# Attention: exponentials times values as one plain float32 matmul in place of three on split parts

## The chip, the cores and the metric

The kernel runs on one core of one Trainium2 chip. The metric is the device time of one execution in microseconds (us), lower is better. A core has TensorE (PE in the profile, with its weight loads as PEld), VectorE (DVE), ScalarE (ACT), GpSimd (POOL) and SyncE (SP), which here issues the DMAs. Each engine works through its own instructions in order; semaphores join them.

## The reference

A trunk of two layers on 512 latent and 256 context tokens of 1024 channels. In each layer one input projection feeds three mixers (a delta rule called RWKV-7, multi-head latent attention, an mLSTM); their outputs go through one output projection, then a SwiGLU network. All of it is float32. What the change touches is the softmax attention of 8 heads, with 96 channels for keys and queries and 64 for values:

```python
def attend(q, keys, vals):
    s = jnp.einsum('bhqd,bhkd->bhqk', q, keys).astype(jnp.float32) * (MLA_QK ** -0.5)
    p = jax.nn.softmax(s, axis=-1)
    return jnp.einsum('bhqk,bhkd->bhqd', p.astype(vals.dtype), vals)
...
    keys = jnp.concatenate([kl, kc], axis=2)
    vals = jnp.concatenate([vl, vc], axis=2)
    out = lax.map(lambda q_blk: attend(q_blk, keys, vals), qb)
...
    if ctx_out:
        oc = attend(qc, kc, vc)
```

Latent queries see all 768 keys, context queries the 256 context keys. Layer 1 has no context output.

## The kernel before

Most large matmuls are done on split operands: a float32 number is held as a high and a low part of type float32r, 12 significant bits each, and a product is three matmuls: high by high, high by low, low by high (the helper mm3, and the loop in gemm at line 263). The projections, the feed-forward network and both matmuls of attention work so. The delta rule and the mLSTM use plain float32 matmuls.

Within a layer come, in this order: the first norm, the input projection with the delta rule, the mLSTM with the attention's up-projections beside it (mla_up), the attention (mla_attend), the output projection (add, on pages of y), the second norm and the feed-forward network.

In mla_up keys and queries are made by token, normalised, rotated, transposed and sent to DRAM by head. At its end the values are made: for each of 6 tiles of 128 tokens the up-projection's PSUM tile (up) is copied by ScalarE to a high part (line 974) and subtracted by VectorE to a low part (line 975). A head has 96 columns of a value tile, 64 of values and 32 of ones (zeros in the low parts), so that the sum of a query's weights comes out of the same matmul.

In mla_attend a head's keys and queries are loaded and split (load, tiles k; lines 996 to 1000), one head ahead. The maximum of each query's scores is taken first (maxima): a matmul on the high parts alone into tile mx (line 1014), a reduction by VectorE into mr (line 1016), a transpose by matmul into pt (line 1020), and a copy by ScalarE into row 96 of the queries (line 1021), so that the scores come out with the maximum subtracted. Then attend goes over the key tiles, 6 for latent queries (512 columns) and 2 for context queries (256 columns, layer 0 alone): three matmuls for the scores (tile st, lines 1034 to 1036, two PSUM buffers), the exponential on ScalarE (line 1038, tile pe), the exponential's split (lines 1040 and 1041), and three matmuls into po (lines 1043 to 1045), which gathers a head's output over its key tiles. In even tiles VectorE copies and subtracts; in odd tiles ScalarE copies and GpSimd subtracts (the patterns in SPLIT). At the end of a range the sums go through a transpose, a reciprocal and a broadcast transpose (lines 1050 to 1058), and VectorE multiplies the outputs (line 1061, tile y).

The maxima of the next head are woven in between the key tiles, two steps for each (the generator ahead), and one step of the delta rule's output (rwkv_post, tiles yt, ph, pst; lines 751 to 782) follows each head but the last. Within these dependencies the order on each engine is made by the framework, which schedules the whole program on a simulated time line before it is built; an edit in one place can so move instructions in others. Layer 0 has 8 x (6 wide + 2 narrow) tiles of exponentials, layer 1 has 8 x 6 wide ones, 112 in all.

Of the kernel before, what the change touches and what calls it, by code (L numbers as in the profile page):

```python
# [24 lines left out]
SPLIT = ('va', 'vg')  # L25
QN = 2
EB = 3
# [18 lines left out]
PARTS = (8, 7, 7)     # hidden tiles taken at a time  # L46
# [6 lines left out]
# tiles of the input projection: 0-1 r, 2-3 k, 4-5 v, 6 wd, 7 ad, 8 gd | 9-12 cq, 13-14 ckv,  # L53
# 15 rotary key and gates | 16 q, 17 k, 18-19 v, 20-21 o
N_IN = 22

# columns of the per-channel parameters
# [9 lines left out]
# the modulation's tiles: on TensorE (layer 0), on VectorE  # L67
MOD_PE = [m for k in range(5) for m in (k, KD + k)]
MOD_DVE = [(0, m) for m in range(48) if m not in MOD_PE] + [(1, m) for m in range(48)]
FIRST = (0, 1, 2, 5, 3, 6, 4, 7)      # the order of the first norm's pages  # L70


def constants():
# [6 lines left out]
    # decay products of the delta rule: rows are key tokens s, columns (P | R) query tokens t  # L80
# [11 lines left out]
    # the upper right quarters of the diagonal blocks of 32 and 64  # L92
    lev = [(s // l == t // l) & (s % l < l // 2) & (t % l >= l // 2) for l in (32, 64)]
    c["c_lev"] = np.tile(np.stack(lev, 1), (2, 1, 1)).astype(f)
    # partition 32 g + 4 q + b holds column block b of row block 2 (g % 2) + i: masks of the diagonal ones
# [16 lines left out]
def pack(inp):  # L112
# [4 lines left out]
    def cm(w, width=P):  # L117
        """[..., K, M] -> [..., M / width, 128, K / 128, width]"""
        *b, K, M = w.shape
        w = w.reshape(*b, K // P, P, M // width, width)  # L120
        n = len(b)
        return np.ascontiguousarray(w.transpose(*range(n), n + 2, n + 1, n, n + 3))

    def km(w):
        """[..., K, M] -> [..., 128, K / 128, M]"""
# [16 lines left out]
    # the delta rule's output channels go (head parity, head pair, channel)  # L142
# [35 lines left out]
def trunk(ctx, tc, I, out, dbg=None):  # L178
# [35 lines left out]
    def rsqrt(dst, src, w, tag):  # L214
        """dst = src ** -0.5 for [128, w] float32 tiles: a step of third order, then one of Newton's"""
# [5 lines left out]
        ve.scalar_tensor_tensor(dst, t, 5.0, dst, ALU.add, ALU.mult)       # 8 / 3 of the root  # L221
# [4 lines left out]
    def split(hi, lo, src, en=ve):  # L226
        """src = hi + lo, both in 12 significant bits"""
# [3 lines left out]
    def weight(src, k, m, en=ve):  # L231
        """[128, k, m] weights from DRAM, as their two parts"""
# [7 lines left out]
    def pages(n, order=None):  # L240
        """n pages of 768 tokens, each in two parts"""
# [3 lines left out]
    def mm3(o, a, b, start, stop):  # L245
        """o += a^T b for split operands"""
# [4 lines left out]
    KORD = (0, 1, 6, 7, 2, 3, 4, 5)     # attention comes last  # L251
# [4 lines left out]
    def gemm(pool, parts, act, ranges, order=None):  # L256
        """W^T act by ranges of tokens: (psum, first, last); parts: [(hi, lo, first k)], act[k] = (hi, lo)"""
# [9 lines left out]
    def gemm_both(pools, ws, act, order):  # L267
        """two output tiles' W^T act over all tokens, page by page of act: their [(psum, first, last)]"""
# [17 lines left out]
    def mod_pe(k, wk, bufs, pool):  # L286
        """layer 0's shift and scale of page k on TensorE"""
# [16 lines left out]
    def silu_rows(wk, pm):  # L304
        """silu(c), silu(c_ctx) on all partitions"""
# [10 lines left out]
    def mod_dve(l, m, cb, t, wk, bufs):  # L316
        """a layer's projection m of c on VectorE"""
# [7 lines left out]
    def gain(l, which, a=0, b=KD):  # L325
        """g * (1 + scale) of one of a layer's two norms, pages a to b"""
# [5 lines left out]
    def norm_stat(acc, X, k, a, b, tmp, en):  # L332
        """acc += the squares of X's page k"""
# [7 lines left out]
    def norm_scale(acc, rng, pm, tag="ss", bufs=1):  # L341
        """1 / rms of ranges of tokens, on all partitions: [(psum, first, last)], and the last operation"""
# [18 lines left out]
    def norm_page(l, which, X, h, bc, k, a, b, tmp):  # L361
        """the modulated norm of X's page k, tokens a to b, into the split page of h"""
# [15 lines left out]
    def pads(z):  # L378
        """the zeros around the latent (1-512) and the context tokens (514-769)"""
# [3 lines left out]
    def shift(t, z, u, c, n):  # L383
        """t += c * (left neighbour + right neighbour)"""
# [12 lines left out]
    def joint(a0, a1):  # L397
        """the like views a0 and a1 of one tile as one view, [partitions, 2, ...]"""
# [3 lines left out]
    def rwkv_in(l, ctx_out, h, rp, rq, tp, pm, pc, early, each):  # L402
        """the projection's tiles for the delta rule, shifted; unit keys, values by token, bonus"""
# [437 lines left out]
    def mla_up(l, ctx_out, lat, wk, vp, pm, krt, post, marks):  # L841
# [123 lines left out]
        for vs, x in ((his, 1.0), (los, 0.0)):  # L965
            for v in vs:
                gp.memset(v[:, :, :, 64:96].bitcast(F32), x)
# [584 lines left out]
```

## Time and profile before

| | |
|---|---|
| median of 3 runs | 2311.01 us (2308.34 to 2317.83) |
| the profiled execution: span from first to last instruction | 2302.2 us |
| busy in it: TensorE, VectorE, ScalarE, GpSimd | 2157.2, 1474.2, 876.9, 381.9 us |
| as shares of the span | 94%, 64%, 38%, 17% |
| mean granted TensorE clock over the span | 0.956 |

The page gives the span of the profiled execution and no time of its own around it; the median of the runs is 8.8 us above the span, the lowest run 6.1 us. A granted clock of 1.0 is 2.4 GHz and 0.5 is 1.2 GHz, the two levels of TensorE's clock; values between are means over a stretch. A matmul's duration in the trace reaches over the start of the next, so a matmul's price is read from one start to the next, not from its duration. A plain float32 matmul of the program shows as two records, each with its weight load.

### The profile page before, as it was taken

The page shows a single profiled execution, that of the slowest core. Times are in us where ns is not written, and L with a number is a line of the kernel's source. Part 1 is how long each engine was busy: PE and PEld are TensorE (multiplying, and loading weights), DVE is VectorE, ACT ScalarE, POOL GpSimd, SP SyncE. Part 2 cuts the span into 40 slices and gives each one's busy share as a digit, 9 for nine tenths or more (in the row PEclk, how much of TensorE's full clock was granted, in tenths as well). Part 3 has the DMA queues.
Part 4 walks back from the last instruction along what each step waited for, and adds up shares of the span by engine and source line. Part 5 has one row for each costly group of instructions (what it writes and reads, how often), then busy time and mean ns, then how long its engine had stood idle before and what let it go on. Part 6 is the DMA issues. An engine that isn't in the chain of part 4 may idle for free.

```text
span 2302.2 us, 36903 instructions
## 1 busy us (share of the span) xinstructions
PE 2157.2 (94%) x14716; PEld 1804.8 (78%) x14716; DVE 1474.2 (64%) x2830; ACT 876.9 (38%) x1583; POOL 381.9 (17%) x544
## 2 busy tenths in 40 slices
PE   6999997987989999999999989999797998999999
PEld 3788886775778888888888878887685677888887
DVE  6687777986767766545444455788798855433333
ACT  4433333654653522122122254434474554222221
POOL 1022332333431100000000111123143421000000
PEclk9999997896899999999999999999797998999999
DMA  7341112231006244333432311211231122333333
GB/s 287 94 141 61 61 41 88 59 103 38 27 11 211 75 136 135 123 118 123 144 127 68 114 60 57 79 52 43 84 106 51 35 64 91 93 97 96 96 97 101
DMA packets 87355, 212.02 MB, mean 92 GB/s; under 512 B 10248, under 2 KB 33680, under 8 KB 86544
## 3 DMA queue, kind: packets, MB, share of 16 engines
q1 hardware_dynamic: 87184, 209.67, 28.6%
q8 instruction: 115, 1.88, 0.3%
q14 instruction: 56, 0.46, 0.1%
HBM read 187.62 MB, written 22.02 MB: 91 GB/s over the span
## 4 chain that ended last, share of the span: by engine, by line
PE 79%; DVE 13%; ACT 3%; DMA 3%; issue 2%; POOL 1%; SPq 0%; DVEq 0%; ACTq 0%; POOLq 0%
PE gm L263 57%; PE psm L586 2%; PE inv L661 2%; PE st L1034 1%; DVE cT L321 1%; DVE mr L1016 1%; PE st L1035 1%; PE mx L1014 1%; DVE wl L229 1%; PE st L1036 1%; PE psm L515 1%; PE po L1045 1%; PE pB L701 1%; DMA wd<-in_mod_d 1%; PE psm L574 1%
## 5 line engine op out<-in xcount | busy, mean ns | idle before, releaser
L263 PE MATMUL gm<-hpage,wh 128*128 128x512 f32 (+1 forms) x3744 | 994.6, 353 | 15.4 <-ACT hpage L228 10.6
L263 PEld LDWEIGHTS gm<-hpage,wh 128*128 128x128 f32 x3744 | 660.1, 190 | 118.2 <-ACT hpage L228 13.0
L263 PE MATMUL gm<-hpage,wl 128*128 128x512 f32 (+1 forms) x1872 | 654.2, 352 | 1.2 <-DVE wl L229 0.9
L228 ACT ACTIVATE wh<-wr 128x1024 fp32r<-128x1024 f32 (+2 forms) x214 | 221.6, 1036 | 556.2 <-PE gm L263 457.7
L263 PEld LDWEIGHTS gm<-hpage,wl 128*128 128x128 f32 x1872 | 355.4, 190 | 49.6 <-DVE wl L229 2.2
L229 DVE TENSOR_TENSOR wl<-wr,wh 128x1024 fp32r<-128x1024 f32 (+2 forms) x214 | 257.7, 1204 | 180.8 <-ACT wh L228 178.8
L263 PE MATMUL gm<-hid,wh 128*128 128x512 f32 (+1 forms) x1056 | 282.6, 356 | 0.0
L263 PEld LDWEIGHTS gm<-hid,wh 128*128 128x128 f32 x1056 | 185.5, 188 | 32.3
L263 PE MATMUL gm<-hid,wl 128*128 128x512 f32 (+1 forms) x528 | 187.4, 356 | 0.0
L1344 DVE SCALAR_TENSOR_TENSOR X<-gm,mod,X 128x512 f32<-128x512 f32 (+1 forms) x100 | 64.2, 643 | 192.0 <-PE gm L263 187.3
L321 DVE CUSTOM_DVE_ANT_0 cT<-wd,cB,mod_b 128x1024 f32<-128x1024 f32 x140 | 177.1, 1294 | 0.4
L1514 DVE SCALAR_TENSOR_TENSOR ft<-ft,gm 128x512 f32<-128x512 f32 x66 | 39.5, 598 | 153.2 <-PE gm L263 153.1
L339 POOL TENSOR_TENSOR acc<-acc,sq 128x512 f32<-128x512 f32 (+1 forms) x15 | 22.6, 1517 | 563.0 <-ACT sq L338 563.0
L263 PEld LDWEIGHTS gm<-hid,wl 128*128 128x128 f32 x528 | 99.0, 188 | 16.1
L1041 POOL TENSOR_TENSOR pe<-pe,pe 128x512 fp32r<-128x512 f32 (+1 forms) x56 | 71.1, 1270 | 135.4 <-ACT pe L1071 107.0
L228 ACT ACTIVATE hid<-ft 128x512 fp32r<-128x512 f32 x66 | 36.2, 549 | 130.5 <-DVE ft L1514 130.5
L1038 ACT ACTIVATE pe<-st 128x512 f32<-128x512 f32 (+1 forms) x112 | 62.8, 563 | 60.8 <-PE st L1036 52.5
L1016 DVE TENSOR_REDUCE mr<-mx 128x1 fp32r<-128x768 f32 (+1 forms) x80 | 67.6, 845 | 20.4 <-PE mx L1014 19.9
L1512 ACT ACTIVATE ft<-gm 128x512 f32<-128x512 f32 x66 | 33.9, 514 | 89.9 <-PE gm L263 89.9
L1014 PE MATMUL mx<-k,k 96*128 96x256 f32 (+1 forms) x144 | 48.6, 414 | 16.5 <-DVE mr L1016 15.4
L586 PE MATMUL psm<-pr,kb 64*128 64x128 f32 (+1 forms) x384 | 55.7, 300 | 1.6 <-POOL pr L556 1.0
L229 POOL TENSOR_TENSOR hpage<-hu,hpage 128x256 fp32r<-128x256 f32 (+1 forms) x32 | 31.9, 1000 | 149.5 <-ACT hpage L228 148.8
(438 smaller groups left out, 3472.0 us busy)
## 6 DMA issues: line engine op xcount, KB each, us to landing
wr<-in_ffn_in SPq DMA_DIRECT2D x88, 512.0 KB, 3.5
wd<-in_mod_d SPq DMA_DIRECT2D x86, 512.0 KB, 4.1
wr<-in_w_in SPq DMA_DIRECT2D x44, 512.0 KB, 3.6
wr<-in_ffn_out SPq DMA_DIRECT2D x34, 448.0 KB, 3.4
wr<-in_w_out SPq DMA_DIRECT2D x20, 512.0 KB, 3.6
wr<-in_ffn_out SPq DMA_DIRECT2D x16, 512.0 KB, 3.6
zs<-ze SPq DMA_DIRECT2D x26, 256.0 KB, 2.0
X<-in_xT SPq DMA_DIRECT2D x16, 384.0 KB, 6.1
```

What stands on the lines that cost most here:

```text
L228: ac.activation(hi, src, AF.Copy)
L229: return en.tensor_tensor(lo, src, hi.bitcast(F32), ALU.subtract)
L263: pe.matmul(ps, x[:, j], act[k][y][:, a:b], start=(i == 0 and n == 0), stop=(i == len(kl) - 1 and n == 2))
L321: ve.tensor_tensor_reduce(out=t[:, s], in0=w, in1=cb[:, s], scale=1.0, scalar=modb[:, l, m:m + 1], op0=ALU.mult, op1=ALU.add, accum_out=mo ...
L586: pe.matmul(pa[j][:, p, c], flat(kb[hr, d, p, c]), flat(pr[hr, d, p, c, 0:nq]), start=True, stop=True)
L661: i = pe.matmul(v8(o)[hr, q], a[hr, d, p, c], b[hr, d, p, c], start=True, stop=True)
L1014: pe.matmul(ps[:, a - k0:b - k0], qh[0:96, n * P:(n + 1) * P], kh[0:96, a:b], start=True, stop=True)
L1016: ve.tensor_reduce(mr[:, n - q0:n - q0 + 1], ps[:, :T - k0], AX.X, ALU.max)
L1038: ac.activation(e, ps, AF.Exp, scale=QK_SCALE)
L1041: engine(1)(el, e, eh.bitcast(F32), ALU.subtract)
L1344: return ve.scalar_tensor_tensor(X[:, m, a:b], ps, mods[l][:, 24 * which + 16 + m, s:s + 1], X[:, m, a:b], ALU.mult, ALU.add)
L1514: ve.scalar_tensor_tensor(t2, t2, 0.5, pup, ALU.mult, ALU.mult)
```

## The change

The split of the exponentials and of the values goes. The values are one float32 tile (three pages of the pool hpage in place of five and one of the pool vl, which goes too), with ones beside each head's 64 columns. A key tile's exponentials go straight into one float32 matmul with them. The exponentials' tile pe has six buffers in place of three, since the two parts beside it are gone. Comments are gone as well; line numbers move by a few. The core of the diff:

```diff
-SPLIT = ('va', 'vg')
 QN = 2
-EB = 3
+EB = 6
...
-        his = [hp.tile([P, 2, 8, 96], F32R, name="hpage") for _ in range(3)]
-        los = [vp.tile([P, 2, 8, 96], F32R, name="vlow")] + [hp.tile([P, 2, 8, 96], F32R, name="hpage") for _ in range(2)]
-        for vs, x in ((his, 1.0), (los, 0.0)):
-            for v in vs:
-                gp.memset(v[:, :, :, 64:96].bitcast(F32), x)
-        V = [(his[n // 2][:, n % 2], los[n // 2][:, n % 2]) for n in range(NT)]
+        vs = [hp.tile([P, 2, 8, 96], F32, name="hpage") for _ in range(3)]
+        for v in vs:
+            gp.memset(v[:, :, :, 64:96], 1.0)
+        V = [vs[n // 2][:, n % 2] for n in range(NT)]
         wt = up_weight("ukv", 2, 512, 1024)
         for n in range(NT):
             ps = up(ckv, wt, n, 512)
-            hi, lo = (v[:, :, 0:64] for v in V[n])
-            src, r = ps.rearrange("p (h b) -> p h b", h=8), rkv[:, n:n + 1]
-            ac.activation(hi, src, AF.Copy, scale=r)
-            ve.scalar_tensor_tensor(lo, src, r, hi.bitcast(F32), ALU.mult, ALU.subtract)
+            ac.activation(V[n][:, :, 0:64], ps.rearrange("p (h b) -> p h b", h=8), AF.Copy, scale=rkv[:, n:n + 1])
...
                 e = wk2.tile([P, 512], F32, name="pe", bufs=EB)[:, :w]
                 ac.activation(e, ps, AF.Exp, scale=QK_SCALE)
-                eh, el = (wk2.tile([P, 512], F32R, name=f"pe{i}", bufs=EB)[:, :w] for i in range(2))
-                engine(0)(eh, e)
-                engine(1)(el, e, eh.bitcast(F32), ALU.subtract)
-                vh, vl = (v.rearrange("p h c -> p (h c)")[:, v0:v0 + P] for v in V[kt])
-                pe.matmul(po[:, :w], vh, eh, start=(kt == kts[0]), stop=False)
-                pe.matmul(po[:, :w], vl, eh, start=False, stop=False)
-                pe.matmul(po[:, :w], vh, el, start=False, stop=(kt == kts[-1]))
+                v = V[kt].rearrange("p h c -> p (h c)")[:, v0:v0 + P]
+                pe.matmul(po[:, :w], v, e, start=(kt == kts[0]), stop=(kt == kts[-1]))
                 yield
...
-        vp = rstack.enter_context(pool(f"vl{l}", 1, "right"))
```

What the schedule makes of it is seen best at the seam between two heads of layer 0 on TensorE. Before (in this order pt<-c_id,yt, pt<-c_id,ph and pt<-wa,g are a step of the delta rule's output, mx a maximum's matmul, pt<-idr,mr its transposes, pt<-one,row the transposes of the sums, st scores, po products):

```order
L1014 MATMUL mx<-k_6699,k_6706 128x512
L1014 MATMUL mx<-k_6699,k_6706 128x256
L772 MATMUL pt<-c_id,yt 128x128
L773 MATMUL pt<-c_id,ph 128x128
L774 MATMUL pt<-wa,g_6059 128x128
L772 MATMUL pt<-c_id,yt 128x128
L773 MATMUL pt<-c_id,ph 128x128
L774 MATMUL pt<-wa,g_6059 128x128
L1045 MATMUL po<-pe_6817,hpage 128x512
L1014 MATMUL mx<-k_6699,k_6706 128x256
L1020 MATMUL pt<-idr,mr 128x128 x6
L1053 MATMUL pt<-one_79,row 128x1 x4
```

The changed kernel at the like seam of layer 0 on TensorE (its line 1008 is 1014 above, 1014 is 1020, 1034 the product, 1042 is 1053):

```order
L771 MATMUL pt<-c_id,yt 128x128
L772 MATMUL pt<-c_id,ph 128x128
L773 MATMUL pt<-wa,g_5996 128x128
L771 MATMUL pt<-c_id,yt 128x128
L772 MATMUL pt<-c_id,ph 128x128
L773 MATMUL pt<-wa,g_5996 128x128
L1034 MATMUL po<-pe,hpage 128x512 x2
L1008 MATMUL mx<-k_6641,k_6648 128x512
L1008 MATMUL mx<-k_6641,k_6648 128x256
L1014 MATMUL pt<-idr,mr 128x128 x6
L1008 MATMUL mx<-k_6641,k_6648 128x256
L1042 MATMUL pt<-one_79,row 128x1 x4
```

A pair of matmuls for a maximum has moved from ahead of the delta rule's step to right ahead of the six transposes, which take its result, and two whole products stand between that step and the maximum where one third of a product stood.

## Rows read from the trace of the kernel before

**Rows 1.** The page's 2nd part: granted clock, tenths, 40 slices of 57.6 us

```profile
PEclk9999997896899999999999999999797998999999
```

**Rows 2.** Stretches: length, busy us (instructions) by engine, granted clock, DMA share, GB/s

```profile
490.00:513.00 23.00, 19.27 (x101) 16.27 (x99) 22.17 (x73) 12.31 (x22) 8.77 (x14) 0.93 0.23 70
533.00:690.00 157.00, 140.29 (x647) 111.29 (x647) 115.56 (x198) 91.36 (x175) 60.90 (x51) 0.86 0.07 20
1750.00:1875.00 125.00, 108.12 (x469) 81.95 (x468) 99.12 (x146) 74.55 (x130) 54.59 (x42) 0.89 0.15 45
1812.00:1875.00 63.00, 55.27 (x276) 42.46 (x275) 50.79 (x72) 42.04 (x74) 27.40 (x22) 1.00 0.16 50
```

**Rows 3.** TensorE in order of time, layer 0: start, length in us

```profile
542.46 0.40 PE L1045 MATMUL po<-pe,hpage 128*128 128x512 f32 x1
542.69 0.39 PE L1043 MATMUL po<-pe,hpage 128*128 128x512 f32 x1
```

**Rows 4.** TensorE's waits, 533 to 690 us: total us, times, longest

```profile
PE po L1045 <- DVE pe L1041: 4.5, 4, 1.6
PE pt L1020 <- DVE ph L781: 2.8, 4, 0.8
PE mx L1014 <- DVE mr L1016: 2.8, 3, 1.8
PE pt L1020 <- DVE mr L1016: 2.1, 3, 1.3
```

**Rows 5.** The same view, 1750 to 1875 us

```profile
PE mx L1014 <- DVE mr L1016: 5.1, 5, 2.2
PE pt L1020 <- DVE mr L1016: 2.8, 1, 2.8
PE po L1045 <- DVE pe L1041: 2.5, 2, 1.8
```

**Rows 6.** VectorE's groups, 533 to 690 us: busy us, mean ns, idle before

```profile
L1016 DVE TENSOR_REDUCE mr<-mx 128x1 fp32r<-128x768 f32 x28 | 26.7, 952 | 5.0 <-PE mx L1014 4.7
L1041 DVE TENSOR_TENSOR pe<-pe,pe 128x512 fp32r<-128x512 f32 x24 | 17.3, 722 | 1.0
L1040 DVE CAST pe<-pe 128x512 fp32r<-128x512 f32 x24 | 16.4, 681 | 12.0 <-ACT pe L1038 10.4 <-PE po L1044 1.5
L1041 DVE TENSOR_TENSOR pe<-pe,pe 128x256 fp32r<-128x256 f32 x8 | 8.9, 1111 | 0.2
```

**Rows 7.** The same view, 1750 to 1875 us

```profile
L1041 DVE TENSOR_TENSOR pe<-pe,pe 128x512 fp32r<-128x512 f32 x24 | 23.2, 966 | 1.0
L1040 DVE CAST pe<-pe 128x512 fp32r<-128x512 f32 x24 | 13.4, 559 | 10.2 <-ACT pe L1038 10.0
```

**Rows 8.** In order of time, layer 0: one stall; in brackets idle before

```profile
651.11 2.08 DVE L1041 TENSOR_TENSOR pe<-pe,pe 128x256 fp32r<-128x256 f32 x1
...
653.25 0.39 PE L1045 MATMUL po<-pe,hpage 128*128 128x256 f32 x1 [1.57 <-DVE pe L1041]
```

**Rows 9.** Stretches as in rows 2: a start, and after that stall

```profile
533.00:541.00 8.00, 7.55 (x20) 6.09 (x20) 3.19 (x6) 3.08 (x6) 1.28 (x1) 0.50 0.00 0
655.00:657.00 2.00, 2.00 (x7) 1.62 (x6) 1.97 (x4) 0.60 (x1) 0.91 (x1) 0.50 0.00 0
```

**Rows 10.** Line 1043: durations ns min/median/max, first and last start, forms

```profile
L1043 PE MATMUL po<-pe,hpage x112: 279/396/629, 537.9 to 1871.0; 128*128 128x512 f32 x96, 128*128 128x256 f32 x16
```

**Rows 11.** TensorE in order of time, layer 1: the mLSTM's plain float32 scores

```profile
1679.00 1.02 PE L1270 MATMUL pss<-ze,hpage 128*128 128x512 f32 x2
1679.85 0.60 PE L1307 MATMUL pbc<-mva,kd 128*128 128x260 f32 x2
```

**Rows 12.** Line 975, the values' low parts, as in rows 10

```profile
L975 DVE SCALAR_TENSOR_TENSOR hpage<-up,rkvn,hpage x8: 740/744/751, 504.9 to 1734.0; 128x512 fp32r<-128x512 f32 x8
```

**Rows 13.** VectorE in order of time, layer 1: ends of two heads

```profile
1812.44 0.67 DVE L1061 TENSOR_TENSOR y<-y,pt 64x512 f32<-64x512 f32 x1
...
1875.11 0.69 DVE L1061 TENSOR_TENSOR y<-y,pt 64x512 f32<-64x512 f32 x1 [0.81 <-PE pt L1058]
```

More of the change, by code (lines that the diff above doesn't have):

```diff
@@ L839, in latent, with mla_up @@
         return parts, rs
-    def mla_up(l, ctx_out, lat, wk, vp, pm, krt, post, marks):
+    def mla_up(l, ctx_out, lat, wk, pm, krt, post, marks):
         steps = iter(POST)
@@ L1061, in attend @@
             done.append((i, ve.tensor_tensor(yo, yo, bc[hr, :w], ALU.mult)))
-        used = {}
-        def engine(use):
-            i = used[use] = used.get(use, -1) + 1
-            en = SPLIT[use][i % len(SPLIT[use])]
-            if use:
-                return {"v": ve, "g": gp}[en].tensor_tensor
-            return {"a": lambda o, x: ac.activation(o, x, AF.Copy), "v": ve.tensor_copy, "g": gp.tensor_copy}[en]
         ranges = ((0, 4, 0), (4, 6, 512))[:2 if ctx_out else 1]
@@ L1441, in trunk @@
             post = rwkv_post(l, ctx_out, data, y, wp2, psum)
-            V = mla_up(l, ctx_out, lat, wk, vp, pm, krt, post, marks)
+            V = mla_up(l, ctx_out, lat, wk, pm, krt, post, marks)
         lstack.close()
```

## The prediction, made before the changed kernel ran

> **What bounds the kernel now.** Read the page first, then the stages that the change touches. On the page the granted clock is full in most slices of 57.6 us; it dips in the seventh to eleventh (345 to 633 us) and again in the thirty-first (1727 to 1784 us), which are around the two attentions [rows 1]. The exponentials-times-values products are all in line 1043 and the two lines after it, so two stretches matter, 533 to 690 us (layer 0) and 1750 to 1875 us (layer 1) [rows 2]. Their mean granted clock is 0.86 and 0.89, and VectorE is busy 115.6 of 157 us and 99.1 of 125 us. TensorE is called busy 140.3 and 108.1 us, but that counts overlapping durations and half-clock work, so it does not say how much it needs.
>
> What it needs comes from start times. At the full granted clock, 2.4 GHz, a 512-column matmul on float32r parts starts 0.23 us after the one before it [rows 3]. A layer 0 head has 36 of them in scores and products (two lots of 6 tiles by 3), 12 with 256 columns, and maxima, transposes and the delta rule's steps beside them. By 0.23 us and its half for 256 columns, the 112 tiles' scores and products need 96 x 6 x 0.23 + 16 x 6 x 0.12 = 144 us, of the 282 us of the two stretches. The rest is the other matmuls, half-clock time and waits. The waits of TensorE show which: the third product waits for the VectorE subtraction of line 1041, the maxima and their transposes (lines 1014, 1020) wait for VectorE's reduction, and the transposes of line 1020 wait for a delta-rule step in tile ph [rows 4, 5]. VectorE works in order, so much of the wait for a reduction is a wait for what was queued ahead of it, and the split of the exponentials is a large part of that queue [rows 6, 7]. One stall shows the whole mechanism: a 256-column subtraction takes 2.08 us from 651.11, the product behind it starts at 653.25 after 1.57 us of idle, and two microseconds later the granted clock is 0.50 [rows 8, 9].
>
> **The change part by part.** The sum is made against the profiled execution, whose span is 2302.2 us. The median of the runs shown, 2311.0 us, lies 8.8 us above that span; I take this difference as unchanged and add the sum to the median. A measurement of this kernel tells 0.5% (11.6 us) from no change.
>
> *The product.* Each of 112 tiles (96 with 512 columns, 16 with 256) [rows 10] loses three float32r matmuls and gains one plain float32 matmul. The mLSTM scores of line 1270 are a plain float32 matmul of the same 128 x 128 by 128 x 512 shape: one is two records in the trace, and what follows starts 0.85 us after the first [rows 11]. So 0.85 against 3 x 0.23 = 0.69: +0.16 us per wide tile. 96 x 0.16 = 15.4, and 16 x 0.08 = 1.3 for the narrow ones, scaled by columns (an estimate): **+16.7 us** at full clock. At half clock everything doubles; at today's mean clocks about a quarter of the time is at half clock (1 - 0.86 = 0.14, half rate, so 28%), which makes it 21; I take 19 because I expect less half-clock time. The Trainium skill, FP8 and Floating Point Precision, section TensorE Precision Notes, says that true float32 takes four passes through the array, against one for the truncated form. By that rule a tile would cost 4 x 0.23 = 0.92, the price would be about 24 us at full clock in place of 16.7, and the sum below would end 7 us higher, near 2305; the same shape was timed in this run [rows 11], so the sum goes by that.
>
> *The exponentials' split.* ScalarE or VectorE no longer copies the exponentials to float32r, VectorE or GpSimd no longer subtracts. VectorE sheds 17.3 + 16.4 + 8.9 us in the first stretch and 23.2 + 13.4 in the second [rows 6, 7], 79 us together. None of it is a saving by itself: only what TensorE waited for is. Directly waited for: 4.5 us (four times) in layer 0 and 2.5 us in layer 1 [rows 4, 5]. These waits cannot happen any more: **-7**.
>
> *The queue on VectorE.* Waits for the reduction (tile mr): 2.8 + 2.1 us in layer 0, 5.1 + 2.8 in layer 1 [rows 4, 5], 12.8 in all. VectorE loses over a third of its work there, but the reduction's own 0.95 us [rows 6] stays between a maximum and its transpose. Bounds: 0 and 12.8; I take 60%: **-8**.
>
> *A wait that is added.* The order of TensorE at the head's seam, quoted ahead, now has a maximum right in front of the six transposes that need its reduction; two whole products stand ahead of that maximum and cover the wait for ph (2.8 us, four times, [rows 4]). In its place comes a reduction of 0.95 us, four times: 3.8 - 2.8 = **+1**. Behind it wait the next scores, which need row 96 of the queries from those transposes.
>
> *The clock.* Time lost at half clock: (1 - 0.86) x 157 = 22 and (1 - 0.89) x 125 = 13.8 us, 36 at most. Idle time is in that, and so is the low clock with which each attention starts (0.50 from 533 to 541 us, before any product is late [rows 9]); by an estimate, 4 us for each start and 6 for idle time, about 22 is left. A split stall brings a low stretch on [rows 8, 9]; others follow waits for the reduction. Bounds: 0 and 22; I take 60%, as for the queue that causes them: **-13.5**.
>
> *The values' split.* Twelve VectorE instructions of 0.74 us, eight of them in the row and four more on tile vlow [rows 12], 8.9 us, leave the stretch before attention, where VectorE was busy 22.2 of 23 us in layer 0 [rows 2]. Some of them lie beside TensorE's up-projections, so bounds 0 and 8.9; half: **-4.5**. Memsets of the low parts, two fewer pages and one fewer pool cost or give nothing: no wait on a page of the values is in any row that I read. Twice the buffers for the exponentials (3 to 6) give nothing either: with two PSUM tiles for the scores, ScalarE can't run further ahead.
>
> *Elsewhere* the order changes only by neighbours; the output projection after attention in layer 0 starts when attention ends, so what is won passes through.
>
> Sum: 19 - 7 - 8 + 1 - 13.5 - 4.5 = **-13 us**; 2311 - 13 = **2298**.
>
> **The rivals.** *No change* (0.33). The direct waits and the values' split give 7 + 4.5 us, the price is 19 + 1, and the reduction's wait and the low clock stay because their cause is the chain maximum, reduction, transpose, row of the queries, which the change doesn't touch: +8.5, 2319.5. Or half of the two 60% terms comes: -2, 2309. For it: the reduction's waits are the longest ones left in layer 1. Against it: VectorE's queue is where they are made.
>
> *Slower* (0.15). TensorE is already what bounds, and each head pays its 6 x 0.16 = 1 us. The place is the second half of layer 1's attention: from 1812.4 to 1875.1 five heads end [rows 13], 12.5 us each at a granted clock of 1.00 [rows 2], where scores, products and maxima alone take 36 x 0.23 + 4 x 0.35 = 9.7 (a maximum is one matmul of 512 columns and one of 256). There the change costs about 5 us and has 3 to give back. If the first halves go the same way, 21 is paid at today's clock, the direct waits turn into waits for the reduction at the seams (+4 more), and only the values' 4.5 comes back: +20.5, 2331. It decides when the queue and the clock together return 8.5 us: there the change breaks even, and each us less is a us slower.
>
> *Much faster* (0.12 of the 0.52 below). All the waits go and the clock stays full: 16.7 - 7 - 12.8 - 22 - 8.9 = -34, 2277; the low clock at each start may shorten as well, by up to the 4 us each, so down to about 2268. Against it: the reduction's 0.95 us stays, and at the seam the order now puts it between two neighbours on TensorE.
>
> **How the numbers follow.** My forecast with the much faster case has 0.52, no change 0.33, slower 0.15; the forecast is over the 0.5% by little, which is why no change has a third. The range, 2268 to 2320, runs from the much faster end to the upper end of no change, leaving out most of the slower case and a little of the faster.
>
> **What would show it.** Right: line 1034 of the changed kernel has 224 records with starts 0.43 us apart; the granted clock of the two attention stretches rises over 0.92; layer 0's attention is shorter by 8 to 12 us and layer 1's first three heads by most of the rest, while the last five get no shorter; no TensorE wait names a subtraction of exponentials. Wrong: the clock stays at 0.86 and 0.89 with waits for the reduction as long as before (then no change), or the product's starts lie 0.46 us apart or more, or the last five heads of layer 1 grow by more than 1 us each (then slower).

## The result, and the profile after

The changed kernel takes 2280.8 us (median of 4 runs, 2277.9 to 2283.6) beside 2309.7 us of the kernel before (4 runs, 2303.9 to 2317.8). The ratio is 0.9868, 95% interval 0.9847 to 0.9890: 1.3% faster, 29 us, where 13 were forecast. The profiled execution of the changed kernel is its slowest of the four and that of before was its fastest, so the two spans, 2302.2 and 2281.8 us, lie only 20.4 us apart. The 8.8 us between span and median before, which the prediction took as fixed, are mostly this: that run took 2303.9 us, 1.7 above its span.

The page of the changed kernel, its granted clock and two groups (line 1010 is the reduction, 1016 before; 1034 the product):

```profile
PEclk9999997897999999999999989999697998999999
...
L1010 DVE TENSOR_REDUCE mr<-mx 128x1 fp32r<-128x768 f32 (+1 forms) x80 | 67.9, 848 | 83.8 <-PE mx L1008 83.6
L1034 PE MATMUL po<-pe,hpage 128*128 128x512 f32 (+1 forms) x224 | 112.2, 590 | 0.5 <-ACT pe L1032 0.4
```

The reduction's group before:

```profile
L1016 DVE TENSOR_REDUCE mr<-mx 128x1 fp32r<-128x768 f32 (+1 forms) x80 | 67.6, 845 | 20.4 <-PE mx L1014 19.9
```

There are 224 records for 112 products, and next to nothing is waited for in front of them. VectorE now sits idle for 83.6 us until a maximum comes from TensorE, where it was 19.9. The two attentions of the changed kernel, from the first scores to the first matmul of the output projection, columns as in [rows 2]:

```profile
533.86:673.20 139.34, 131.27 (x595) 91.50 (x596) 68.99 (x137) 76.00 (x148) 25.04 (x19) 0.97 0.08 22
1738.44:1855.36 116.92, 110.49 (x424) 70.90 (x425) 58.44 (x100) 60.69 (x106) 22.34 (x18) 0.93 0.16 48
```

The same two stretches of the kernel before, by the same marks:

```profile
533.45:693.21 159.76, 142.83 (x659) 113.06 (x660) 116.14 (x201) 93.72 (x180) 60.90 (x51) 0.86 0.07 19
1749.24:1874.76 125.52, 108.64 (x471) 82.19 (x469) 99.49 (x147) 74.55 (x130) 54.59 (x42) 0.89 0.15 45
```

Layer 0's attention is 20.4 us shorter and layer 1's 8.6, 29.0 together, as much as the medians lie apart; from one profile of each kernel, that it fits so closely is luck. VectorE's work in them falls from 215.6 to 127.4 us, and the granted clock goes from 0.86 and 0.89 to 0.97 and 0.93. Between the two attentions the changed kernel took 1065.2 us and the kernel before 1056.0; in the profiles of the twelve kernels below that stretch takes 1058.6 to 1076.1, so those 9 us are what hides a part of the gain in the two spans. But for the values' split of layer 1 the engines do the same work there; the granted clock is 0.98 before and 0.96 in the changed kernel, and why it differs is not shown.

TensorE's waits in the two attentions of the changed kernel (533 to 673, 1738 to 1855 us; total us, times, longest), beside [rows 4, 5]:

```profile
PE pt L1014 <- DVE mr L1010: 3.4, 6, 0.9
PE st L1028 <- ACT k L1015: 1.9, 3, 0.8
PE mx L1008 <- DVE mr L1010: 1.1, 2, 0.9
...
PE st L1028 <- ACT k L1015: 2.3, 6, 0.9
PE pt L1042 <- ACT row L1039: 1.8, 6, 0.7
PE pt L1014 <- DVE mr L1010: 0.9, 2, 0.5
PE mx L1008 <- DVE mr L1010: 0.6, 1, 0.6
```

The first three lines are layer 0's, the others layer 1's. The waits for the reduction were 12.8 us and are 6.0, or 5.1 without 0.9 that lies ahead of the first scores, and none is longer than one reduction; those of the transposes for the delta rule's step, and those for a subtraction of exponentials, are gone. The price of the product is near the forecast's 0.85 us. In order of time on TensorE, two products a key tile apart, at full clock:

```profile
541.71 1.02 PE L1034 MATMUL po<-pe,hpage 128*128 128x512 f32 x2
...
543.27 1.02 PE L1034 MATMUL po<-pe,hpage 128*128 128x512 f32 x2
```

They start 1.56 us apart; with three scores at 0.23 us, 0.69 in all, 0.87 is left for a product. VectorE in layer 1, ends of two heads, beside [rows 13]:

```profile
1790.38 0.67 DVE L1050 TENSOR_TENSOR y<-y,pt 64x512 f32<-64x512 f32 x1
...
1854.70 0.69 DVE L1050 TENSOR_TENSOR y<-y,pt 64x512 f32<-64x512 f32 x1 [0.81 <-PE pt L1047]
```

From the third head's end to the last one's, five heads, it is 64.3 us, before 62.7: that is where the forecast saw no gain, and there is none. The clock was full there before too [rows 2], so the whole gain lies where it was not.

### The profile page after: what moved, and what is told of

Read it like the earlier page. It is cut to its first block, busy times and chain, and to the rows that moved or that the text cites. A ratio compares the mean times of both kernels' runs of the same rounds, so it can differ in the third digit from the quotient of the medians.

```text
span 2281.8 us, 36365 instructions
## 1 busy us (share of the span) xinstructions
PE 2159.2 (95%) x14604; PEld 1780.9 (78%) x14604; DVE 1381.9 (61%) x2706; ACT 844.7 (37%) x1527; POOL 314.2 (14%) x482
## 4 chain that ended last, share of the span: by engine, by line
PE 81%; DVE 10%; ACT 4%; DMA 2%; issue 2%; POOL 1%; SPq 0%; DVEq 0%; ACTq 0%; POOLq 0%
PE gm L262 57%; PE po L1034 4%; PE psm L585 2%; PE inv L660 2%; PE st L1028 1%; DVE cT L320 1%; PE st L1029 1%; PE st L1030 1%; PE mx L1008 1%; PE psm L514 1%; PE pB L700 1%; DVE wl L228 1%; PE psm L573 1%; ACT hu L365 1%; PE up L246 1%
## 5 line engine op out<-in xcount | busy, mean ns | idle before, releaser
L1010 DVE TENSOR_REDUCE mr<-mx 128x1 fp32r<-128x768 f32 (+1 forms) x80 | 67.9, 848 | 83.8 <-PE mx L1008 83.6
L1034 PE MATMUL po<-pe,hpage 128*128 128x512 f32 (+1 forms) x224 | 112.2, 590 | 0.5 <-ACT pe L1032 0.4
L227 ACT ACTIVATE hid<-ft 128x512 fp32r<-128x512 f32 x66 | 36.2, 549 | 128.4 <-DVE ft L1492 128.4
L1028 PE MATMUL st<-k,k 97*128 97x512 f32 (+1 forms) x112 | 78.0, 698 | 4.7 <-ACT k L1015 4.1
```

The source lines that it names most:

```text
L227: ac.activation(hi, src, AF.Copy)
L1010: ve.tensor_reduce(mr[:, n - q0:n - q0 + 1], ps[:, :T - k0], AX.X, ALU.max)
L1028: pe.matmul(ps, kh[0:97, ks], qh[0:97, qs], start=True, stop=False)
L1034: pe.matmul(po[:, :w], v, e, start=(kt == kts[0]), stop=(kt == kts[-1]))
```

## The experiments

The theory after the result: the product costs what it was forecast to cost, and VectorE's relief brings more than forecast, through shorter waits and a clock that stays up. Rivals: the matmul's form gives the time back, or the direct wait alone did it. Every kernel is scheduled anew. TensorE's order in the attentions is nearly that of the changed kernel in eb3, vlow, qpool and warm; in the others it differs, above all in layer 0, and a step's time holds what that does too. Medians, in the order of the runs; the kernel before had 2311.6, 2312.6, 2312.8 and 2317.7 us in the four sets (marked 1 to 4).

| kernel | what it is | median us | ratio to before, 95% |
|---|---|---|---|
| waits (1) | one float32 product behind the split's queue and wait | 2333.3 | 1.0062 to 1.0113 |
| queue (1) | changed, with the split made and unread | 2311.0 | 0.9974 to 1.0009 |
| twice (1) | changed, each product twice | 2358.1 | 1.0173 to 1.0219 |
| one (1) | changed, product as one float32r matmul | 2246.1 | 0.9694 to 0.9739 |
| nowait (2) | before, nothing waits for a subtraction | 2303.6 | 0.9946 to 0.9985 |
| three (2) | before, no split of exponentials, three products | 2271.2 | 0.9785 to 0.9840 |
| eb3 (2) | changed, three buffers | 2281.6 | 0.9834 to 0.9881 |
| vlow (2) | changed, values' low parts made and unread | 2279.3 | 0.9816 to 0.9867 |
| qdve (3) | changed, VectorE's part of the split, unread | 2288.1 | 0.9875 to 0.9931 |
| qpool (3) | changed, ScalarE's and GpSimd's part, unread | 2290.9 | 0.9875 to 0.9930 |
| warm (3) | changed, unread matmuls ahead of attention | 2290.3 | 0.9870 to 0.9921 |
| two (4) | three, without its third product | 2257.2 | 0.9715 to 0.9796 |

**waits and queue.** The changed kernel with the split's instructions back, and the product behind them or not (both, and qdve and qpool, with three buffers for the exponentials; 'eb3' tries that alone):

```diff
                 ac.activation(e, ps, AF.Exp, scale=QK_SCALE)
+                eh = wk2.tile([P, 512], F32R, name="pe0", bufs=3)[:, :w]
+                el = wk2.tile([P, 512], F32, name="pe1", bufs=3)[:, :w]         # queue: F32R
+                count[0] += 1
+                if count[0] & 1:
+                    ve.tensor_copy(eh, e)
+                    ve.tensor_tensor(el, e, eh.bitcast(F32), ALU.add)       # queue: subtract
+                else:
+                    ac.activation(eh, e, AF.Copy)
+                    gp.tensor_tensor(el, e, eh.bitcast(F32), ALU.add)       # queue: subtract
...
-                pe.matmul(po[:, :w], v, e, start=(kt == kts[0]), stop=(kt == kts[-1]))
+                pe.matmul(po[:, :w], v, el, start=(kt == kts[0]), stop=(kt == kts[-1]))  # queue: e
```

> Here the product is one plain float32 matmul, as changed, but it reads the result of a copy and a two-operand step that run where the split ran (VectorE for one tile, ScalarE and GpSimd for the next), so queue and direct wait are those of before; the step adds instead of subtracting, which doubles weights and sums alike. The values have no low part. Theory A (the price of the matmul is real, and what came back is VectorE's queue, the direct wait and the clock that follows them): before plus 16 to 19 for the product, less up to 4.5 for the values, 2320 to 2330 us, attention clocks about 0.86 and 0.89 as before. Rival B (the matmul's form gives the time back, since one long matmul covers waits and keeps the clock up): 2285 to 2300 us, clocks 0.93 or more in both attentions.

> As the kernel 'waits' of this set, but the matmul reads the exponentials themselves; the copy and the subtraction are made and nobody reads them. VectorE's, ScalarE's and GpSimd's queues are as before, the direct wait is gone. Theory A: the direct wait gives 7 us and a part of the clock, so 10 to 15 us under 'waits', about 2312 us, and over 25 above the changed kernel, with waits of maxima and transposes for the reduction near 13 us. Rival C (the direct wait alone carried it, the queue nothing): as the changed kernel, 2278 to 2286 us.

Measured: 2333.3 us, 22 above before and 3 above the range of theory A; and 2311.0 us, 30 above the changed kernel, as A said, though 22 under 'waits' and not 10 to 15. The waits for the reduction in 'queue' are 11.7 us. Rival C falls: the direct wait alone does not carry the gain. Against rival B 'waits' says less than it seems to, since here the whole product stands behind the second step, where before the first two thirds did not. Its waits in layer 0:

```profile
PE po L1043 <- DVE pe L1038: 7.7, 9, 1.6
PE po L1043 <- POOL pe L1041: 2.6, 2, 2.4
```

That is 10.3 us, against 4.5 and 0.3 before. The attentions of 'queue':

```profile
540.39:691.43 151.04, 136.24 (x596) 93.97 (x596) 110.73 (x201) 93.83 (x180) 61.85 (x51) 0.94 0.07 20
1767.56:1891.05 123.49, 113.44 (x425) 73.10 (x426) 98.33 (x148) 75.05 (x131) 55.64 (x42) 0.91 0.16 46
```

Of what parts 'queue' from the changed kernel in the profiles, 18 us lie in the attentions, 6.5 ahead of the first and 11 between them, in the longest such stretch of all, 1076.1 us, where its clock is 0.95 beside 0.96.

**nowait and three.** A cleaner way through the same steps, from the other end: the kernel before with one word changed, then without the split.

```diff
-                pe.matmul(po[:, :w], vh, el, start=False, stop=(kt == kts[-1]))
+                pe.matmul(po[:, :w], vh, eh, start=False, stop=(kt == kts[-1]))
```

```diff
-                e = wk2.tile([P, 512], F32, name="pe", bufs=EB)[:, :w]
-                ac.activation(e, ps, AF.Exp, scale=QK_SCALE)
-                eh, el = (wk2.tile([P, 512], F32R, name=f"pe{i}", bufs=EB)[:, :w] for i in range(2))
-                engine(0)(eh, e)
-                engine(1)(el, e, eh.bitcast(F32), ALU.subtract)
+                eh = wk2.tile([P, 512], F32R, name="pe", bufs=EB)[:, :w]
+                ac.activation(eh, ps, AF.Exp, scale=QK_SCALE)
```

> The kernel before, with one word changed: the third product takes the high part of the exponentials again in place of the low part, so the low part of the exponentials is left out of the result, and the subtraction runs on and nobody reads it. Three matmuls as before, queue as before, no wait for a subtraction. If the waits counted in the profile of before were all that hung on the subtraction (8 us with GpSimd's), 8 us under before, 2303 us. If such a wait costs several times what it shows, because TensorE's clock falls behind it (the sum gave the clock 13.5 us for the whole change; 'waits' and 'queue' lay 22 us apart), 15 to 22 us under before, 2289 to 2297 us.

> The kernel 'nowait' of this set without the split of the exponentials: the exponential writes float32r itself, and three products take it; the low part of the exponentials is left out, the values' split stays. From 'nowait' to here is VectorE's queue alone ('queue' to the changed kernel: 30 us by the medians, 18 in the two attentions); from here to the changed kernel is the price of the product alone, less the values. Theory: price 15 to 19 us, so 2262 to 2268 us. If the plain float32 matmul also keeps the clock up, as it may since 'one' fell to 0.88 and 0.84 and 'twice' rose to 0.99 and 0.97, the price on the path is less: 2268 to 2281 us.

Measured: 2303.6 and 2271.2 us. The direct wait is worth 9 us, about what was counted, and the queue 32; 'three' comes out in the second of its two cases, so the price on the path is less than 15 us. 'three' and 'vlow', which came from one set and both make the values' low parts, differ in the product and the buffers: 8 us, half of the price at full clock. From 'three' to the changed kernel it is 10.

With 'queue' and the changed kernel these two make a square, and none of the four waits for a subtraction (in 'nowait' the products still wait for the copy). The queue costs 32 us with three products and 30 with one; the one product costs 7 us with the queue and 10 without. So by the medians the long matmul pays back hardly more where there are waits to cover, and rival B falls. In the attentions of the profiles there is more for it: those of 'queue' are 5.2 us shorter than those of 'nowait', at a higher clock, and what makes 'queue' the slower program lies outside them (between the attentions 1076.1 us beside 1061.1). Those are one profile each, and that of 'queue' was its slowest run of ten. The two attentions of 'nowait', then those of 'three':

```profile
533.45:686.20 152.75, 137.47 (x660) 110.26 (x660) 114.53 (x201) 94.09 (x180) 61.86 (x51) 0.87 0.07 20
1747.27:1874.26 126.99, 111.42 (x470) 86.20 (x469) 100.68 (x147) 74.01 (x130) 55.20 (x42) 0.85 0.15 44
```

```profile
534.17:670.54 136.37, 127.09 (x660) 104.56 (x660) 68.27 (x137) 75.92 (x148) 23.96 (x19) 0.92 0.08 22
1732.30:1844.20 111.90, 104.25 (x474) 81.69 (x472) 59.09 (x100) 60.65 (x106) 22.61 (x18) 0.91 0.17 50
```

Length times granted clock says what a stretch would take at full clock (an estimate: idle time at half clock is halved too, and the clock's two digits leave about 1.4 us in a sum). Both attentions together:

| | length | at full clock | lost to the clock |
|---|---|---|---|
| before | 285.3 | 249.1 | 36.2 |
| nowait | 279.7 | 240.8 | 38.9 |
| three | 248.3 | 227.3 | 21.0 |
| changed | 256.3 | 243.9 | 12.4 |

So taking the queue away gives 13.5 us of work and waits and 17.9 of clock. The product then costs 16.6 us at full clock, the 16.7 of the forecast, and the clock is higher by 8.6 us: 8.0 us of length. eb3 and vlow have the changed kernel's matmuls, and by their attentions it is 15.7 and 18.9 us at full clock with 7.2 and 8.9 back, so that 16.6 lies so near is luck.

The mean granted clock of the whole program is known for every run. By span and clock in the same way, averaged over a kernel's runs, 114 us are lost before, 110 in 'nowait', 89 in 'three', 88 in the changed kernel, 94 in eb3 and 84 in vlow. What the queue costs in clock is seen there again. What the product brings back is seen in vlow, and not in the other two: in their profiles the stretch between the attentions lost about what the attentions got (its clock is 0.97 in 'three' and vlow, 0.96 in those two). That the product costs half of its price is shown by the medians; that the clock pays the other half is shown for the attentions alone.

Without the direct wait, and with the queue, TensorE waits longer for the reduction. In 'nowait', layer 0 and then layer 1:

```profile
PE mx L1014 <- DVE mr L1016: 6.5, 4, 4.7
PE pt L1020 <- DVE mr L1016: 2.3, 5, 0.6
...
PE mx L1014 <- DVE mr L1016: 9.1, 5, 3.4
PE pt L1020 <- DVE mr L1016: 1.2, 3, 0.5
```

That is 19.1 us, against 12.8 before and 5.7 in 'three'.

**one, two and twice.** The same VectorE work, and other products; with the low parts left out as the expectations say.

```diff
-                pe.matmul(po[:, :w], v, e, start=(kt == kts[0]), stop=(kt == kts[-1]))
+                pe.matmul(po[:, :w], v, e, start=(kt == kts[0]), stop=False)
+                pe.matmul(po[:, :w], v, e, start=False, stop=(kt == kts[-1]))
```

```diff
-        vs = [hp.tile([P, 2, 8, 96], F32, name="hpage") for _ in range(3)]
+        vs = [hp.tile([P, 2, 8, 96], F32R, name="hpage") for _ in range(3)]
...
-                e = wk2.tile([P, 512], F32, name="pe", bufs=EB)[:, :w]
+                e = wk2.tile([P, 512], F32R, name="pe", bufs=EB)[:, :w]
```

The first diff is 'twice', the second 'one'; 'two' is 'three' with its third matmul (vh, eh) left out.

> The changed kernel with each product issued twice into the same sum (weights and their sums double together). 112 tiles, 96 at 0.86 us and 16 at 0.43, are 89 us. Theory A (TensorE sets the pace in both attentions): 85 to 92 us more, about 2369 us, clock at 0.97 or more in both attentions. Rival D (TensorE waits for maxima and loads often enough to hide a part, 15 us of waits are left in the changed kernel): 60 to 78 us more, 2341 to 2359 us.

> The changed kernel with exponentials and values rounded to float32r where they are made and one float32r matmul for the product; the low parts of both are left out. A wide tile's product goes from 0.86 to 0.23 us, 66 us over the 112 tiles. Theory A: if TensorE sets the pace throughout, 2281 - 66 = 2215 us; since then the maxima's chain and ScalarE come close to bounding, 2215 to 2240 us. Rival D (what is freed turns into waits for the reduction and a lower clock): over 2250 us, attention clock below 0.9.

> The kernel 'three' without its third product: exponentials written as float32r, high part of the values and low part of the values by them. The low part of the exponentials is left out, values keep both parts. At full clock that is 0.23 us less for each of 96 wide tiles and 0.12 for each of 16 narrow ones, 24 us, under 'three'. If a product's time lies on the path and the clock stays where 'three' has it (0.92 and 0.91): 2247 us. If the granted clock falls as TensorE has less to do between the same waits ('one' with a single matmul had 0.88 and 0.84 and 2246 us): half of it comes, 2256 to 2262 us.

Measured: 2358.1, 2246.1 and 2257.2 us. 'twice' costs 77 us for 89 us of matmuls: rival D's upper figure, so a seventh of the added work is not seen; the clock is theory A's. In the attentions it is 82.0 us more at full clock and 6.0 less lost to the clock, so filled waits and the clock hide about as much each. 'one' lies between the two forecasts, with the clock that D named. 'two' is 14 us under 'three' for 24 us less work, the length that the second case named, but not for its reason: in the profiles its attentions are 18 us shorter, with the clock of 'three' but for 0.02 in layer 1. (The profile of 'two' is its fastest run, 3 us under the median.) The attentions of 'one', 'two' and 'twice':

```profile
535.04:656.07 121.03, 107.07 (x531) 86.37 (x531) 65.98 (x137) 76.06 (x148) 25.98 (x19) 0.88 0.09 25
1723.08:1824.33 101.25, 90.64 (x380) 69.25 (x380) 58.63 (x100) 60.30 (x107) 22.43 (x18) 0.84 0.19 55
```

```profile
532.82:658.86 126.04, 116.14 (x595) 94.45 (x596) 66.82 (x137) 76.08 (x148) 24.91 (x19) 0.92 0.08 24
1718.64:1822.78 104.14, 94.06 (x423) 72.65 (x422) 59.09 (x100) 60.47 (x106) 22.37 (x18) 0.89 0.18 54
```

```profile
538.00:717.90 179.90, 175.50 (x723) 113.89 (x724) 67.98 (x137) 76.09 (x148) 25.22 (x19) 0.99 0.06 17
1778.43:1930.76 152.33, 145.32 (x516) 86.54 (x517) 57.21 (x96) 61.17 (x106) 22.49 (x18) 0.97 0.13 37
```

VectorE is busy for 66 to 69 and 57 to 59 us in all five kernels of this kind. With 0.23, 0.46, 0.69, 0.86 and 1.72 us of product in a wide tile ('one', 'two', 'three', changed, 'twice') layer 0's clock is 0.88, 0.92, 0.92, 0.97 and 0.99, layer 1's 0.84, 0.89, 0.91, 0.93 and 0.97; what both lose to the clock is 30.7, 21.5, 21.0, 12.4 and 6.4 us, so it is not only that a longer stretch thins out the same loss. 'one' and 'two' are faster than both kernels, and 'three' too, but they are another computation: all three leave out the low part of the exponentials, and 'one' that of the values.

**eb3 and vlow.** The buffers alone; and the values' low parts (with their pages and zeros) made as before and read by nobody.

```diff
-EB = 6
+EB = 3
```

```diff
...
-            ac.activation(V[n][:, :, 0:64], ps.rearrange("p (h b) -> p h b", h=8), AF.Copy, scale=rkv[:, n:n + 1])
+            src, r, hi, lo = ps.rearrange("p (h b) -> p h b", h=8), rkv[:, n:n + 1], V[n][:, :, 0:64], los[n // 2][:, n % 2, :, 0:64]
+            ac.activation(hi, src, AF.Copy, scale=r)
+            ve.scalar_tensor_tensor(lo, src, r, hi, ALU.mult, ALU.subtract)
```

> The changed kernel with three buffers for the exponentials as before, in place of six. The prediction's step: no difference (within 3 us of 2281). The rival: the deeper buffer lets ScalarE run ahead and gives a part of the gain, 2286 us or more without it.

> The changed kernel with the values' low parts made again by VectorE, with their pages and zeros, and read by nobody. The prediction's step: 4.5 us more (0 to 8.9), 2285 us. The rival, by the changed kernel's trace, in which layer 0's attention starts 0.4 us later than before: 0 to 2 us more.

Measured: 2281.6 and 2279.3 us, both within the runs of the changed kernel. Neither the buffers nor the values' split makes a difference that the runs can tell; the prediction's 4.5 us for the latter is not there.

**qdve and qpool.** Of the split in 'queue' one branch of the two; here 'qdve' against 'queue', and 'qpool' has the other branch alone.

```diff
                 if count[0] & 1:
                     ve.tensor_copy(eh, e)
                     ve.tensor_tensor(el, e, eh.bitcast(F32), ALU.subtract)
-                else:
-                    ac.activation(eh, e, AF.Copy)
-                    gp.tensor_tensor(el, e, eh.bitcast(F32), ALU.subtract)
```

> The changed kernel with VectorE's part of the split alone, read by nobody: in every other tile VectorE copies the exponentials to float32r and subtracts; ScalarE and GpSimd do nothing of the kind. 'queue', with both parts, was 30 us above the changed kernel by the medians, 18 of it in the two attentions. If VectorE's queue in front of the reductions carried that, 2300 to 2311 us. If GpSimd's subtractions carried it (they slow VectorE, or hold a buffer), 2281 to 2288 us.

> The other half: in every other tile ScalarE copies and GpSimd subtracts, read by nobody, and VectorE has no part of the split. If VectorE's queue carried it: 2281 to 2288 us, by ScalarE's 0.63 us copies at most a few us. If GpSimd and ScalarE carried it: 2300 to 2311 us.

Measured: 2288.1 and 2290.9 us, 7 and 10 above the changed kernel, where both together are 30: 'qdve' at the upper end of its second case, 'qpool' in neither. In the attentions, 'qdve' is 9.5 us longer, 'qpool' 2.4 and 'queue' 18.3; most of what 'qpool' costs lies outside them and is not explained. Neither half carries it; together they cost more than their sum. It is the same with VectorE's busy time in the attentions: 127.4 us in the changed kernel, 54.6 more in 'qdve', 9.5 more in 'qpool', 81.6 more in 'queue'. VectorE's groups show where. In 'queue', then in 'qdve' (1037 copies, 1038 subtracts, 991 is the keys' low part):

```profile
L1038 DVE TENSOR_TENSOR pe<-pe,pe 128x512 fp32r<-128x512 f32 x48 | 39.7, 828 | 1.0
L1037 DVE CAST pe<-pe 128x512 fp32r<-128x512 f32 x48 | 23.8, 496 | 28.9 <-ACT pe L1032 28.7
L991 DVE SCALAR_TENSOR_TENSOR k<-kq,qkgain,k 96x512 fp32r<-96x512 f32 x8 | 18.7, 2342 | 3.8 <-ACT k L990 3.8
```

```profile
L1038 DVE TENSOR_TENSOR pe<-pe,pe 128x512 fp32r<-128x512 f32 x48 | 33.0, 687 | 1.0
L1037 DVE CAST pe<-pe 128x512 fp32r<-128x512 f32 x48 | 21.5, 448 | 40.2 <-ACT pe L1032 40.0
L991 DVE SCALAR_TENSOR_TENSOR k<-kq,qkgain,k 96x512 fp32r<-96x512 f32 x8 | 9.2, 1147 | 1.9 <-ACT k L990 1.9
```

The same instructions take longer while GpSimd subtracts. VectorE's 112 instructions on exponentials were busy 63.1 us in 'qdve', 73.5 in 'queue' and 83.0 in the kernel before, so 10 to 20 us of that queue went with GpSimd's half. In layer 1 of the kernel before, a copy took 0.42 us on average with GpSimd idle (12 of them) and 0.70 beside one of GpSimd's instructions (12). The stall of [rows 8], read again with GpSimd's rows of the kernel before:

```profile
650.40 1.83 POOL L1000 TENSOR_TENSOR k<-kq,k 96x768 fp32r<-96x768 f32 x1 [0.19 <-DVE pe L1040]
...
652.19 0.72 POOL L1041 TENSOR_TENSOR pe<-pe,pe 128x256 fp32r<-128x256 f32 x1
```

VectorE's subtraction of 2.08 us ends at 653.19, behind both of these; the one that ran with GpSimd idle took 0.41. This agrees with the Trainium skill, SBUF — State Buffer, section Who interferes with whom: a VectorE instruction with two inputs in SBUF, or a copy in its two-port mode, contends with GpSimd for a pair of ports which one of the two holds at a time, and the later one is blocked until the other is done. The section says that a reduction is never held up so on this chip, and those of 768 columns took 0.95 us in all of these kernels.

**warm.** Unread matmuls in the idle time ahead of each attention:

```diff
+                if warm and n > q0:
+                    pe.matmul(fill[:, 0:256], mr[:, n - q0 - 1:n - q0].bitcast(F32).to_broadcast([P, P]),
+                              V[0].rearrange("p h c -> p (h c)")[:, 0:256], start=True, stop=True)
...
+        if l == 0:
+            for _ in range(4):
+                pe.matmul(fill, ident, V[NT - 1].rearrange("p h c -> p (h c)")[:, 0:512], start=True, stop=True)
```

> The changed kernel with matmuls whose results nobody reads put into the idle time ahead of each attention: one plain float32 matmul of 256 columns behind each of the first head's last three maxima, and in layer 0 four of 512 columns while the first loads are awaited. TensorE's granted clock is 0.50 there, and in the changed kernel it stays so until 538 to 543 us and 1743 to 1748 us, well into the first head. If the idle time ahead sets it, the first heads start at full clock: 4 us less in layer 0 and 6 in layer 1, 2271 to 2277 us. If the added matmuls only delay the maxima: 2281 to 2286 us.

Measured: 2290.3 us, 9.5 slower than the changed kernel, above both forecasts. Layer 1's attention got its 5 us (111.7 us at a clock of 0.98); layer 0's did not (141.9 us at 0.95; 530 to 538 us ran at 0.50 all the same). Both attentions started later than in the changed kernel, 4.7 and 13.1 us in the profiles; what made the stretches ahead longer is not shown.

## Why the prediction was right or wrong

The sign and the range held; the size did not. By the medians, which need no estimate of the clock, two steps failed. The product was put at +19 us and costs 8 ('three' to 'vlow') to 10 (to the changed kernel). The two waits on VectorE and the clock behind them were put at -28.5 together, and 'nowait' (-9) and 'three' (-32) show -41, in a set whose kernel before took 3 us more than in the first. The values' split, -4.5, gave nothing. In the forecast's own terms, with the table of lengths and clocks, which holds one profile of each kernel:

- **The product**, +16.7 at full clock: measured +16.6, by eb3 and vlow 15.7 and 18.9. The further 2.3 us that the forecast added for half clock had the wrong sign: with the longer product the attentions lost 8.6 less to the clock. This is the largest error, 10.9 us. The forecast took the clock for something that only waits bring down.
- **The direct waits**, -7: measured -8.3 at full clock, and -9 by the medians of 'nowait'. Right, and in the attentions they brought no clock with them (36.2 and 38.9 lost): that one such stall costs several times what it shows is not borne out here. (In 'waits', where that wait is 17.9 us in both layers, its removal did raise the clock: 0.87 and 0.88, in 'queue' 0.94 and 0.91.)
- **The queue on VectorE**, -8 with bounds 0 and 12.8: measured -13.5, past the upper bound. The 60% itself was right: the waits for the reduction went from 12.8 us to 5.7 in 'three' and 5.1 in the changed kernel. What failed is the bound, which took this wait as if the direct one were another matter. With the direct wait gone and the queue still there, the waits for the reduction were 19.1 us ('nowait'), and taking the queue away took 13.4 of them. Direct waits and queue together were put at -15, and the waits named did go down by 15; but the stretches got 21.8 us shorter at full clock. The other 7 fall in the step to 'nowait', and what they were is not shown.
- **The clock**, -13.5 with bounds 0 and 22: what waits gave is 36.2 - 21.0 = 15.2, near the forecast, and all of it came with the queue. The product's 8.6 on top make 23.8, above the bound. Of the 36 us lost before, 14 were set down as not to be had (starts of the attentions, other idle time); 12.4 are left.
- **The values' split**, -4.5: nothing ('vlow'). Layer 0's attention starts 0.4 us later than before. Its cover, the up-projections, was named but not believed.
- **The seam**, +1: not measured by itself; it is in the product's 16.6. Transposes wait for a reduction 6 times in layer 0, 3.4 us in all, in place of 2.8 for the delta rule's step and 2.1 for a reduction.

The differences are 10.9, 1.3, 5.5, 1.7 and 1 us in favour, less 4.5 for the values: 16 us, from -13 to -29. By places: layer 0 was to win 8 to 12 us and won 20; in layer 1 the first three heads won and the last five did not, as forecast; the clock passed 0.92 in both; the product's two records start 0.43 us apart. The choice of the likeliest case failed with these steps: the much faster case, all waits gone and the clock full, was given 0.12. Its -34 less the 8.9 that it credited to the values is -25; the other 4 are 1.8 of clock past its bound, 1.3 of the direct waits and 0.7 of the queue. It is not that all waits went: 5.1 us of them for the reduction are left.

Three readings in the prediction are off without changing it. The 79 us that VectorE sheds leave out 3.8 of copies of 256 columns; the direct waits leave out 1.0 us behind GpSimd; and at half clock a float32r matmul starts 0.43 us after the one before it, a little less than twice 0.23.

## What to carry to other kernels

A matmul with more work in it can cost less than its time where the clock sags, so price it at full clock, then look at what the clock lost in that stretch, and let the time of whole runs decide. When two engines share a job by halves, look for instructions of one that are longer beside the other: taking the job away returns that time too. And when two waits come from one queue, don't price them one by one: with the first gone a part of it turns up in the second, and only the end of the queue shows what both were worth.

## What the runs showed of the hardware that was not expected

- With VectorE's work alike, a longer product went with a higher granted clock in both attentions, from 0.88 and 0.84 with 0.23 us in a tile to 0.99 and 0.97 with 1.72.
- GpSimd holds VectorE up: the subtraction of the keys' low part (96x512) takes 0.74 us with GpSimd idle, 1.15 us on average in 'qdve' and 2.34 in 'queue'.
- One float32 matmul of 512 columns (0.86 us) replaced three float32r ones (0.69): 16 to 19 us for 112 tiles at full clock, of which the medians show 8 to 10.
